# Queries of a hybrid transformer block from seven half-size products, with combined operands made by accumulating transfers

## The chip, the cores and the metric

The kernel runs on one core of a Trainium2 chip. The metric is device time in microseconds (us). Lower is better.

## What is computed

One layer of a diffusion backbone on 1024 latent tokens and 256 context tokens of 1024 features, in float32. In short (the MLP and the second half of the layer are left out; the change doesn't touch what they compute):

```python
h_x = _modulate(x, g_pre_mix[l], sh1, sc1)          # rmsnorm(x) * gain * (1 + scale) + shift
h_c = _modulate(ctx, g_pre_mix[l], csh1, csc1)
u_x, q_x, k_x, v_x = _project(h_x, w_in[l])         # h @ w_in, four blocks of 512 columns
u_c, q_c, k_c, v_c = _project(h_c, w_in[l])
attn_x = _neighbourhood_attention(q_x, k_x, v_x, k_c, v_c, rpb[l])
mix_x = jnp.concatenate([_pool_mixer(u_x, pool_w[l], pool_scale[l]), attn_x], axis=-1) @ w_out[l]
x = x + gt1 * _rmsnorm(mix_x, g_post_mix[l])
```

The pool mixer takes, in four groups of 128 channels, a sliding mean over 2, 4, 8 or 16 tokens less the token itself, and multiplies it with a 128 x 128 matrix. The attention has 8 heads of 64 features; the shift, scale and gate vectors come from a product of silu(c) with w_mod, 1024 x 6144. The queries are the product of the 1024 x 1024 modulated tokens with 512 columns of w_in, times -1/8 as the kernel keeps them.

## The kernel before

**Precision and tiles.** Each factor of a float32 product is split into a high part (rounded to the matmul's type, by ACT) and a low part (the rest, subtracted by DVE), and each product of two tiles is three matmuls (`three`, L193 to L196): high x high, high x low, low x high. The modulated tokens stand feature-major: `hx[b][k]` is one page of 128 x 1024 elements for half b of the tokens (512) and features 128k to 128k + 127, its left half the high part, its right half the low part. A page is a buffer of the pool `act`, of which there are 33 (L89). Raw weights go through 4 buffers (`wraw`), split weights through 8 (`whl`), so one group of 512 columns of w_in, split, fills all 8.

**Order of the work around the change.** After a start in which the tokens are normalised, turned and modulated, and the keys are formed, come: the context's keys (`pkc`, L565); the values of the context (`pvc`) and of eight tiles of latent tokens (`pv`, L575 to L593); the pool mixer's projection in eight groups (`pu`, L651 to L670), each followed by DVE work on the sliding sums (`pooled`), whose result is split at once into the pages `d`; the queries (`queries`, L704), eight groups `pq{j}_{b}` of 24 matmuls for feature tile j and token half b; and the pool products (`pool_out`, L638: three matmuls for each group and half, then evacuations to `y` and `mix`). Four query groups of token half 0 come first, then `pq0_1`, then the pool products, then `pq1_1`, and the last two groups stand in the first two turns of attention. In between run `background` steps: sums over w_mod for the later vectors, each step one load of 512 KB and one operation of DVE (L209 to L217), some number of them after each group.

**Attention** (L926 on) is a software pipeline over 32 units (head pair j, column block m). A turn forms scores (PE), adds the bias table and takes the maximum (DVE), exponentiates (ACT), turns the result (PE) and multiplies with the values (PE). The bias tables `tab` are made by POOL from a mask and the loaded position bias (L684).

**What sets the order.** A planner orders each engine's instructions from their program order and their readiness in its own time model, hands out buffers and puts in the waits. Inside `in_order(...)` the named engines keep the program's order: PE in the part that starts with `pq0_1` and the pool products (`pooling`), PE, ACT, DVE and SP in attention and before the values. Loads go through SP's queue; accumulating transfers (`add_to`: the destination is read, added to and written by the DMA) through POOL's.

Of the kernel before, what the change touches and what calls it, by code (L numbers as in the profile page):

```python
# [80 lines left out]
def hybrid_block(ctx, tc, x, ctx_in, w_mod, b_mod, gp1, gp2, w_in, pool_w, rpb, w_out, w1, w2, vectors,  # L81
# [61 lines left out]
    def split(src, hi, lo):  # L143
        nc.scalar.copy(hi, src)
        nc.vector.tensor_tensor(lo, src, hi.bitcast(F32), sub)
# [9 lines left out]
    def step_split(src, hi, lo, less=False):  # L155
        if less:
            nc.scalar.activation(hi, src, AF.Copy, scale=-1.0)
        else:
            nc.scalar.copy(hi, src)  # L159

        def second():
            if less:
                nc.vector.scalar_tensor_tensor(lo, src, -1.0, hi.bitcast(F32), mul, sub)
            else:
                nc.vector.tensor_tensor(lo, src, hi.bitcast(F32), sub)  # L165

        if stepwise:
            behind.append(second)
        else:
            second()  # L170
# [6 lines left out]
    def high_low(name, raw):  # L177
        hi = whl.tile([P, 1024], F32R, tag="hl", name=f"{name}h")
        lo = whl.tile([P, 1024], F32R, tag="hl", name=f"{name}l")
        split(raw, hi, lo)  # L180
        return hi, lo

    def weights(name, src):
        return high_low(name, load(name, src))
# [13 lines left out]
    def modulated(tmp, name, src, scale, shift, hi, lo, n, on_act=False):  # L198
        h = tmp.tile([P, 512], F32, tag="t", name=f"{name}t")
        if on_act:  # L200
            nc.scalar.activation(h[:, :n], src, AF.Identity, bias=shift, scale=scale)
            nc.scalar.copy(hi, h[:, :n])
        else:
            nc.scalar.activation(hi, src, AF.Identity, bias=shift, scale=scale)
            nc.vector.tensor_scalar(h[:, :n], src, scale, shift, mul, add)
        nc.vector.tensor_tensor(lo, h[:, :n], hi.bitcast(F32), sub)
# [49 lines left out]
    with tc.tile_pool(name="ps1", bufs=6, space=PSUM) as ps1, tc.tile_pool(name="tmp1", bufs=3) as tmp:  # L256
# [39 lines left out]
        nc.vector.tensor_scalar_add(b_sc, b_sc, 1.0)  # L296
        sT = once("sT", [P, KT, 32])
# [100 lines left out]
        def shift_scale(q, mr):  # L398
# [5 lines left out]
            for v in range(2):  # L404
                nc.vector.tensor_tensor(a1[v][:, hs], pv[:, 1, v], b_sc[:, hs], add)
                nc.vector.tensor_tensor(a1[v][:, hs], a1[v][:, hs], g1c[:, hs], mul)
                nc.vector.tensor_tensor(s1[v][:, hs], pv[:, 0, v], b_sh[:, hs], add)
# [3 lines left out]
        def latent(b, k):  # L411
# [3 lines left out]
                      on_act=(b == 1))  # L415
# [50 lines left out]
        for q in range(4):  # L466
# [3 lines left out]
            if q < 3:  # L470
                mr = mod_rows(q + 1)
                wgt.append(high_low(f"wk{q + 1}", raw_k[q + 1]))
# [78 lines left out]
        def in_group(name, c0):  # L551
            return [weights(f"{name}{kk}", pair(w_in, kk, c0, 512)) for kk in range(KT // 2)]
# [11 lines left out]
        raw_v = [load(f"wv{kk}", pair(w_in, kk, 1536, 512)) for kk in range(KT // 2)]  # L564
# [1150 lines left out]
```

## Time before, and its profile

| | |
|---|---|
| time before, median of 3 runs | 1044.7 us (1044.54 to 1045.26) |
| the profiled execution's own time | 1044.82 us |
| its span, first to last instruction | 1043.0 us |
| PE, DVE, ACT, POOL busy | 99%, 68%, 51%, 9% of the span |
| start of the context's values | 88.1 us |
| start of the pool projection | 144.3 us |
| start of the queries | 189.4 us |
| start of the pool products | 216.7 us |
| first scores | 227.9 us |

The profile is of one execution. PE is the matmul engine, PEld its weight loads, DVE, ACT and POOL the elementwise engines, SP the engine that issues loads. A line number is one of the kernel's; where a helper records an operation (`three`, `split`), every use has the helper's line. "[7.08 <-PE pq L196]" behind a row says that the engine had been idle for 7.08 us before it and that the last thing it waited for was a matmul into `pq`. In a group's row the name before the arrow is written and those behind it are read.

### The profile page before, as it was taken

How to read it: one execution, taken by the hardware profiler on the slowest of the kernel's cores; microseconds unless marked ns; L12 is line 12 of the kernel's file. 1: busy time of each engine (PE TensorE's matmuls, PEld its weight loads, DVE VectorE, ACT ScalarE, POOL GpSimd, SP SyncE). 2: the span in 40 equal slices, each digit the busy share in tenths (PEclk: the TensorE clock that was granted, in tenths of full speed). 3: DMA queues.
4: the chain of work that ended last, by engine and by line, in shares of the span. 5: the costliest groups of instructions: out<-in, count | busy, mean ns of one | idle time of the engine just before them, and what ended most of it. 6: DMA issues, size and time to landing. Idle time of an engine off the chain costs nothing.

```text
span 1043.0 us, 15532 instructions
## 1 busy us (share of the span) xinstructions
PE 1029.6 (99%) x5862; PEld 846.0 (81%) x5862; DVE 711.6 (68%) x1118; ACT 530.8 (51%) x923; POOL 96.4 (9%) x155
## 2 busy tenths in 40 slices
PE   8999999999999999999999999999999999999996
PEld 6788788877888888887888888888888888888885
DVE  5535657536897588878998876764676666547586
ACT  7553121247888465876655555545553334334441
POOL 3010200041331203320000000000000000000001
PEclk9999999999999999999999999999999999999998
DMA  9905764033337696595786553445787766655556
GB/s 341 337 21 178 270 216 135 21 75 100 64 81 189 160 218 203 189 250 167 263 271 231 193 191 129 156 139 192 268 325 264 234 230 222 200 173 194 175 187 201
DMA packets 108155, 199.61 MB, mean 191 GB/s; under 512 B 8496, under 2 KB 45104, under 8 KB 108080
## 3 DMA queue, kind: packets, MB, share of 16 engines
q1 hardware_dynamic: 84544, 152.92, 44.7%
q10 hardware_dynamic: 17136, 30.97, 8.0%
q0 software_dynamic: 6400, 14.72, 6.7%
q8 instruction: 46, 0.75, 0.3%
q14 instruction: 29, 0.24, 0.1%
HBM read 149.81 MB, written 39.34 MB: 181 GB/s over the span
## 4 chain that ended last, share of the span: by engine, by line
PE 96%; ACT 1%; DMA 1%; DVE 1%; issue 0%; SPq 0%; DVEq 0%; POOLq 0%; ACTq 0%
PE pk L433 4%; PE S L753 3%; PE pa L829 3%; PE phv L194 3%; PE phz L194 3%; PE phx L194 3%; PE pyv L196 3%; PE phz L195 3%; PE pyz L196 3%; PE pyx L194 3%; PE phx L195 3%; PE phv L195 3%; PE pyx L196 3%; PE phx L196 3%; PE pyv L194 3%; PE pyz L195 3%
## 5 line engine op out<-in xcount | busy, mean ns | idle before, releaser
L140 POOL TENSOR_TENSOR ry<-vy,nhalf 128x1 f32<-128x1 f32 x8 | 4.4, 551 | 570.8 <-DVE vy L138 570.8
L776 ACT ACTIVATE sp<-sp,nm 128x640 f32<-128x640 f32 (+1 forms) x64 | 51.4, 803 | 9.5 <-DVE nm L767 8.7
L767 DVE CUSTOM_DVE_ANT_0 sp<-S,tab 128x640 f32<-128x640 f32 (+1 forms) x56 | 42.8, 802 | 17.9 <-PE S L753 11.3
L1328 ACT ACTIVATE c<-c 128x512 f32<-128x512 f32 x48 | 30.3, 632 | 46.2 <-DVE c L1448 21.6
L159 ACT CAST wpS<-S 128x512 fp32r<-128x512 f32 x64 | 38.6, 616 | 27.8 <-PE phv L196 9.4
L165 DVE TENSOR_TENSOR wpS<-S,wpS 128x512 fp32r<-128x512 f32 x64 | 43.5, 686 | 10.4 <-ACT wpS L159 10.4
L194 PE MATMUL phx<-thB,wpA 128*128 128x512 f32 x128 | 50.2, 392 | 0.0
L195 PE MATMUL phx<-tlB,wpA 128*128 128x512 f32 x128 | 49.8, 389 | 0.0
L196 PE MATMUL phx<-thB,wpA 128*128 128x512 f32 x128 | 49.8, 389 | 0.0
L1329 ACT ACTIVATE c<-c 128x512 f32<-128x512 f32 x48 | 30.3, 631 | 15.3 <-DVE sa L1411 12.1
L194 PEld LDWEIGHTS phx<-thB,wpA 128*128 128x128 f32 x128 | 24.0, 188 | 5.5 <-ACT s L1379 0.5
L753 PE MATMUL S<-kT,q 64*128 64x384 f32 (+1 forms) x128 | 28.0, 495 | 0.4 <-DVE nm L767 0.4
L196 PEld LDWEIGHTS phx<-thB,wpA 128*128 128x128 f32 x128 | 24.0, 188 | 5.1
L195 PEld LDWEIGHTS phx<-tlB,wpA 128*128 128x128 f32 x128 | 24.0, 188 | 4.8
L829 PE MATMUL pa<-pt,v 128*64 128x128 f32 x352 | 25.9, 279 | 0.7 <-ACT px L809 0.3
L814 DVE COPY pt<-T 128x512 f32<-128x512 f32 x32 | 21.9, 685 | 5.5 <-PE T L795 5.5
L194 PE MATMUL phz<-thB,wpS 128*128 128x512 f32 x64 | 25.0, 391 | 0.0
L194 PE MATMUL phv<-thT,wpA 128*128 128x512 f32 x64 | 25.0, 391 | 0.0
L196 PE MATMUL phv<-thT,wpA 128*128 128x512 f32 x64 | 24.9, 389 | 0.0
L195 PE MATMUL phz<-tlB,wpS 128*128 128x512 f32 x64 | 24.9, 389 | 0.0
L194 PE MATMUL phy<-thT,wpS 128*128 128x512 f32 x64 | 24.9, 389 | 0.0
L195 PE MATMUL phy<-tlT,wpS 128*128 128x512 f32 x64 | 24.9, 389 | 0.0
(1039 smaller groups left out, 3326.3 us busy)
## 6 DMA issues: line engine op xcount, KB each, us to landing
b<-in_w SPq DMA_DIRECT2D x64, 512.0 KB, 4.3
hrS<-hdS SPq DMA_DIRECT2D x32, 512.0 KB, 5.5
hrA<-hdA SPq DMA_DIRECT2D x24, 512.0 KB, 5.6
wm<-in_w_mod SPq DMA_DIRECT2D x16, 512.0 KB, 9.6
wa_0w<-in_w SPq DMA_DIRECT2D x16, 512.0 KB, 5.1
wa_1w<-in_w SPq DMA_DIRECT2D x16, 512.0 KB, 4.2
hdA<-c ACTq DMA_DIRECT2D x32, 256.0 KB, 2.4
hdS<-sa ACTq DMA_DIRECT2D x32, 256.0 KB, 2.6
```

Source lines behind the costliest of these rows:

```text
L159: nc.scalar.copy(hi, src)
L165: nc.vector.tensor_tensor(lo, src, hi.bitcast(F32), sub)
L194: nc.tensor.matmul(ps, ahi, bhi, start=first, stop=False, skip_group_check=more)
L195: nc.tensor.matmul(ps, ahi, blo, start=False, stop=False, skip_group_check=more)
L196: nc.tensor.matmul(ps, alo, bhi, start=False, stop=last, skip_group_check=more)
L433: nc.tensor.matmul(pks[b][j], wk(wgt, k, low, j * P, P), r, start=(k == 0 and n == 0), stop=(k == KT - 1 and n == 2))
L753: nc.tensor.matmul(S[e][:, c0 : c0 + keys.shape[1]], q[hs, cols], keys[hs], start=True, stop=True)
L767: nc.vector.tensor_tensor_reduce(out=to, in0=s, in1=bt, scale=1.0, scalar=BIG, op0=add, op1=ALU.min, accum_out=nm)
L776: nc.scalar.activation(sp, sp, AF.Exp, bias=least[i, e], scale=-1.0, accum_out=sums[i][:, e : e + 1])
L829: nc.tensor.matmul(pa[e * HD : (e + 1) * HD, cols], v[:, f : f + HD], turns[i][:, e, c] if c < 4 else fifths[i][:, :, (e + 1) * HD : (e + ...
L1328: nc.scalar.activation(r, src, AF.Relu)
L1329: nc.scalar.activation(r, r, AF.Square)
```

## The change

The query product is divided in halves three ways. The tokens give four blocks Abk, b the half of the tokens and k the half of the features (512 x 512 each); w_in's query columns give four blocks Bkc, k the half of the features and c the half of the 512 columns. Instead of eight products of blocks, seven are formed (Winograd's form of Strassen's scheme), from

- S1 = A21 + A22, S2 = S1 + A11, S3 = A21 + A11, S4 = S2 + A12, and T1 = B12 + B11, T2 = B22 + T1, T3 = B22 + B12, T4 = T2 + B21, where the second half of the features is kept with its sign turned (in tokens and weights both), which makes differences into sums;
- the products A11 x B11, A12 x B21, S2 x T2, S1 x T1, S4 x B22, S3 x T3, A22 x T4, each of 24 matmuls of 128 x 128 x 512, in this order.

For the sums, the modulated tokens are kept as plain float32 in place (`kept`), written to memory (`tokens`, 8 transfers of 512 KB), and read back into two pages for each S, the further terms added by accumulating transfers. S4 adds S2's raw pages, which lie in the chip's buffer already. The T are formed likewise from w_in in raw weight buffers. Each S is split into four pages. The first five products stand before the pool products in the in-order part; S3 x T3 and A22 x T4 stand in the first two turns of attention, where two query groups stood; `pq1_1` between the pool products and the first scores is gone. The evacuations add or subtract on DVE where they were a scaled copy on ACT.

The pool projection is moved ahead of the values. The values take token half 1 first. The pool differences are kept whole (`differences`) and split only next to the pool products, a group at a time (`difference_split`). Background steps come three at a time in the pool groups and context values, two in the first value groups. One small set of vector operations (`a2`, `less_a2`, `less_s2`) is put behind attention on DVE.

```diff
+    def add_to(to, more):
+        nc.gpsimd.dma_start(to, more, accum_op=add)
...
             modulated(tmp, f"hx{b}_{k}", src, a1[0][:, k : k + 1], s1[0][:, k : k + 1], h[:, :512], h[:, 512:], 512,
-                      on_act=(b == 1))
+                      on_act=(b == 1), kept=src if b == 1 or k > 1 else None)
...
-                wgt.append(high_low(f"wk{q + 1}", raw_k[q + 1]))
+                wgt.append(high_low(f"wk{q + 1}", raw_k[q + 1], 1.0 if q == 0 else -1.0))
...
             if j == 3:
-                wgt = [high_low(f"wv{kk}", raw_v[kk]) for kk in range(KT // 2)]
+                wgt = in_weights("wu", raw_u)
             nc.scalar.copy(kc[:, j], ps)
+
+        tokens = dram.tile([P, KT, SEQ], F32, tag="tokens", name="tokens")
+        for k in range(KT):
+            if k < 2:
+                hi, lo = hx[0][k][:, :512], hx[0][k][:, 512:]
+                nc.vector.tensor_tensor(xT[k][:, :512], hi.bitcast(F32), lo.bitcast(F32), add)
+            nc.sync.dma_start(tokens[:, k], xT[k])
...
+                if g == 3 and b == 0:
+                    raw_v = in_raw("wv", 1536)
+                if g == 3 and b == 1:
+                    wgt = in_weights("wv", raw_v)
+                background(3)
+            differences.append(pooled(g, up).rearrange("p (r m c) -> p m r c", r=QR, m=NM))
...
+        def token_raw(name, first, *more):
+            raw = [page(f"{name}r{i}") for i in range(2)]
+            for i in range(2):
+                nc.sync.dma_start(two(raw[i]), token_half(first, i))
+            for m in more:
+                for i in range(2):
+                    if isinstance(m, str):
+                        add_to(two(raw[i]), token_half(m, i))
+                    else:
+                        add_to(raw[i], m[i])
+            return raw
+
+        def token_operand(name, raw):
+            rows_of[name] = []
+            for i in range(2):
+                hi, lo = page(f"{name}h{i}", F32R), page(f"{name}l{i}", F32R)
+                split(raw[i], hi, lo)
+                rows_of[name] += [(hi[:, o : o + 512], lo[:, o : o + 512]) for o in (0, 512)]
...
+        for n, m in enumerate((4, 5, 6, 7, 0, 1, 2, 3)):
+            ps = bank(f"pv{m}")
+            token_group(ps, wgt, lat_tok(m // 4, m % 4))
...
+            background(2)
+            if n == 2:
+                sraw["S2"] = token_raw("S2", "A21", "A22", "A11")
+            if n == 3:
+                qraw["B11"] = query_raw("B11", "B11")
+                qraw["B21"] = query_raw("B21", "B21")
+                qraw["T2"] = query_raw("T2", "B22", "B12", "B11")
+            if n == 5:
+                token_operand("S2", sraw["S2"])
+                qraw["T1"] = query_raw("T1", "B12", "B11")
...
-        for j in range(4):
-            queries(j, 0, bank(f"pq{j}_0"), (1, 2, 3, 99)[j])
-        mask_page()
-        tables(0)
         with in_order(ET.PE) as pooling:
-            queries(0, 1, bank("pq0_1"), 0)
+            w11, w21 = (query_weights(n, qraw[n]) for n in ("B11", "B21"))
+            x = [bank(f"pqx{j}") for j in range(2)]
+            for j in range(2):
+                query_product(x[j], j, "A11", w11, True)
+                nc.scalar.copy(query(j, 1), by_tile(x[j]))
+            wt = query_weights("T2", qraw["T2"])
+            qraw["B22"] = query_raw("B22", "B22")
+            sraw["S1"] = token_raw("S1", "A21", "A22")
+            for j in range(2):
+                query_product(x[j], j, "A12", w21, False)
+                nc.scalar.copy(query(j, 0), by_tile(x[j]))
+            wt1 = query_weights("T1", qraw["T1"])
+            token_operand("S1", sraw["S1"])
+            sraw["S4"] = token_raw("S4", "A12", sraw["S2"])
+            qraw["T3"] = query_raw("T3", "B22", "B12")
+            qraw["T4"] = query_raw("T4", "B21", "B22", "B12", "B11")
+            y = [bank(f"pqy{j}") for j in range(2)]
+            for j in range(2):
+                query_product(y[j], j, "S2", wt, True)
+                nc.vector.tensor_tensor(query(j, 1), by_tile(y[j]), query(j, 1), add)
+            wb22 = query_weights("B22", qraw["B22"])
+            token_operand("S4", sraw["S4"])
+            mask_page()
+            tables(0)
+            z = [bank(f"pqz{j}") for j in range(2)]
+            for j in range(2):
+                query_product(z[j], j, "S1", wt1, True)
+                nc.vector.tensor_tensor(query(2 + j, 1), query(j, 1), by_tile(z[j]), sub)
+            sraw["S3"] = token_raw("S3", "A21", "A11")
+            wt3 = query_weights("T3", qraw["T3"])
+            difference_split(0)
+            for j in range(2):
+                query_product(z[j], j, "S4", wb22, False)
+                nc.vector.tensor_tensor(query(2 + j, 0), by_tile(z[j]), query(j, 1), sub)
+            wt4 = query_weights("T4", qraw["T4"])
+            token_operand("S3", sraw["S3"])
             for g in range(4):
+                if g < 3:
+                    difference_split(g + 1)
                 pool_out(g)
...
             with tc.issue_after(pooling[ET.PE]):
-                queries(1, 1, bank("pq1_1"), 0)
+                pass
...
                 if i < 2:
-                    queries(2 + i, 1, bank(f"pq{2 + i}_1"), 0)
+
+                    for j in range(2):
+                        query_product(last_queries[j], j, ("S3", "A22")[i], (wt3, wt4)[i], i == 0)
+                    for j in range(2):
+                        to, less = (query(2 + j, 1), query(2 + j, 1)) if i == 0 else (query(j, 1), query(j, 1))
+                        if i == 0:
+                            nc.vector.tensor_tensor(to, less, by_tile(last_queries[j]), sub)
+                        else:
+                            nc.vector.tensor_tensor(to, by_tile(last_queries[j]), less, sub)
```

More of the change, by code (lines that the diff above doesn't have):

```diff
@@ L563, in hybrid_block @@
         kc = kcp.rearrange("p (j t) -> p j t", j=4)
-        raw_v = [load(f"wv{kk}", pair(w_in, kk, 1536, 512)) for kk in range(KT // 2)]
+        raw_u = in_raw("wu", 0)
         for j in range(4):
@@ L673, in hybrid_block @@
+        background(99)
+        vb = [vp[m // 2][:, (m % 2) * 512 : (m % 2) * 512 + 512] for m in range(NM)]
         tabs, msk = [], []
```

141 lines of the change are left out of this document (78 added, 63 removed).

## The prediction

> **What bounds the kernel now.** I read the page's busy table first, then the granted clock, then busy time by stretch around the change, and last the timelines of PE, ACT and DVE and the waits of the queues there.
>
> ```profile
> span 1043.0 us, 15532 instructions
> PE 1029.6 (99%) x5862; PEld 846.0 (81%) x5862; DVE 711.6 (68%) x1118; ACT 530.8 (51%) x923; POOL 96.4 (9%) x155
> core 0: 1043.0 us, clock 0.997
> core 0: us, PE busy (x) PEld busy (x) DVE busy (x) ACT busy (x) POOL busy (x), PEclk, DMA share, GB/s
> 88.00:100.00 12.00, 12.00 (x55) 9.78 (x54) 9.27 (x9) 3.35 (x6) 0.00 (x0) 1.00 0.81 280
> 100.00:112.00 12.00, 12.00 (x59) 9.36 (x58) 9.88 (x8) 1.55 (x3) 0.45 (x1) 1.00 0.92 316
> ...
> 160.00:176.00 16.00, 16.00 (x73) 13.24 (x72) 13.91 (x25) 4.46 (x8) 0.00 (x0) 1.00 0.53 170
> 176.00:189.00 13.00, 13.00 (x64) 10.18 (x63) 4.64 (x9) 3.64 (x4) 1.91 (x4) 1.00 0.13 43
> 189.00:200.00 11.00, 11.00 (x50) 9.13 (x49) 9.06 (x27) 3.39 (x6) 0.00 (x0) 1.00 0.00 0
> 200.00:216.00 16.00, 16.00 (x73) 13.24 (x72) 7.49 (x9) 2.89 (x6) 1.19 (x4) 1.00 0.09 26
> ```
>
> PE has work in 99% of the span, at full clock, and in every stretch from the values to the queries it never waits (12.00 of 12.00, 16.00 of 16.00). The time is therefore the number of matmuls times their pitch, as long as operands stand ready. DMA is nearly full at 100 to 112 (0.92) and empty at 189 to 200 (0.00). A matmul fewer in this part is time saved; a late operand is time lost at once, since PE's order through the products is fixed and holds nothing to run in between.
>
> **The change part by part. Fewer matmuls.**
>
> ```profile
> 189.44 0.39 PE L194 MATMUL pq<-hx,wq0h 128*128 128x512 f32 x1
> ...
> 194.88 0.39 PE L194 MATMUL pq<-hx,wq0h 128*128 128x512 f32 x1
> ...
> 216.65 0.40 PE L194 MATMUL py<-d,pwh 128*128 128x512 f32 x1
> ...
> 222.33 0.39 PE L194 MATMUL pq<-hx,wq0h 128*128 128x512 f32 x1
> ...
> 227.86 0.70 PE L753 MATMUL S<-kcT,q 64*128 64x256 f32 x4
> ```
>
> The first two rows are the starts of two query groups of 24 matmuls: 5.44 us, 0.2267 each (the 0.39 is latency, overlapped). Before: 8 groups, 192 matmuls. After: 7 products of 2 column tiles x 4 feature tiles x 3, 168. That is 24 x 0.2267 = 5.44 us less, all of it ahead of the first scores: before, six groups stood there, now five products; two groups or products follow in attention's first two turns in both. Nothing hides this gain, and the changed order of pools and values costs PE nothing, the same matmuls being issued. The first product thus starts where the first group does, at 189.44 on before's clock.
>
> **The pools ahead of the values.** The background sums now fall on the pool groups, three steps each, together with the pools' DVE work, the 8 writes of the tokens to memory, and the values' weights at the end.
>
> ```profile
> L194 PE MATMUL pvc<-wv0h,hc x4: 389/390/396, 88.1 to 94.4; 128*128 128x512 f32 x4
> ...
> 88.35 0.34 SPq L174 DMA_DIRECT2D wmsh_0w<-in_w_mod  x1
> ...
> 111.28 0.33 SPq L174 DMA_DIRECT2D wmsc_7w<-in_w_mod  x1
> ...
> 186.70 1.06 ACT L144 CAST wq1h<-wq1w 128x1024 fp32r<-128x1024 f32 x1 [0.32 <-PE pu L195]
> ...
> 187.79 1.23 DVE L145 TENSOR_TENSOR wq1l<-wq1w,wq1h 128x1024 fp32r<-128x1024 f32 x1 [0.15 <-ACT wq1h L144]
> ```
>
> Sixteen loads of 512 KB went out in 22.9 us, 1.53 us each, at 280 to 316 GB/s. Between 88 and the values I count 8 token writes, 19 background loads (22 steps, of which three only open a sum) and the 4 loads of the values' weights: 31 x 1.53 = 47.4 us, so the last lands near 135.8. Its split takes 1.06 + 1.23: 138.1. PE comes to this stage at 88.1 (the first row, the values' start before); eight groups end at 131.6, and the fourth weight is read 18 matmuls (4.1 us) later, at 135.7. So PE waits 2.4 if transfers only follow one another, and nothing if the writes find gaps; I take half, 1.2. The upper end is some 9, if DVE (9.88 of 12.00 busy already) works off its queue of sums and pools late, with the weights' subtractions behind them.
>
> **Operands by adding transfers.** S1, S2, S4, S3 are each loaded in two tiles and added to by DMAs of POOL's queue, then split on ACT and DVE into four pages; T1 to T4 likewise in weight buffers. A second accumulation waits in POOL's queue for the first, and whatever is queued there stands behind it (the bias tables among it).
>
> ```profile
> wq1w<-in_w_in SPq DMA_DIRECT2D x1, 512.0 KB, 4.6
> wq3w<-in_w_in SPq DMA_DIRECT2D x1, 512.0 KB, 3.7
> x<-xr POOLq DMA_DIRECT2D x8, 512.0 KB, 4.3
> nf<-nf POOLq DMA_DIRECT2D x2, 512.0 KB, 6.4
> nf<-t POOLq DMA_DIRECT2D x2, 512.0 KB, 8.8
> to_1w<-in_w_out POOLq DMA_DIRECT2D x1, 512.0 KB, 13.2
> ```
>
> A load takes 3.7 to 4.6, I take 4.1. An accumulation: 6.4 and 8.8 for a few at a time, 13.2 on full DMA; a plain store from the same queue 4.3. I take 7.6, midway between the two rows of the same kind and size, keep 4.3 and 13.2 as ends, and 2.3 for ACT and DVE to split. S2, T2 and T1 are ordered in the middle of the values, more than 25 us ahead: I cost them at nothing, DMA having room there (0.53, then 0.13 busy). What counts is when pages come free.
>
> ```profile
> SPq L677 <- PE pq L196: 25.9, 1, 25.9
> POOL tab L682 <- PE pq L196: 24.8, 1, 24.8
> 206.64 1.23 DVE L612 TENSOR_TENSOR sa<-u 128x1023 f32<-128x1023 f32 x1 [7.08 <-PE pq L196]
> ```
>
> Before is already short of its 33 pages here: the mask's load stood 25.9 us and the tables' memset 24.8 until a query group had read its last token page, and a pool sum 7.08. After has more to hold. At the first product I count 12 token pages (A11, A12, A22), 10 of keys and values, 4 differences, 6 of S2: 32 of 33, and the last goes to the queries. So S1's tiles wait for A11's pages, given free by the 15th and 18th matmul of the first product, at 192.8 and 193.5. First half of S1: 192.8 + 4.1 + 7.6 + 2.3 = 206.8; its product is due at 189.44 + 3 x 5.44 = 205.76, its second half, 207.5, is due 6 matmuls later at 207.1. Wait 1.0, product done at 212.2. S4's second tile takes a page of S2, read for the last time 18 matmuls into the third product, 204.4: 204.4 + 4.1 + 7.6 + 2.3 = 218.4, wanted 6 matmuls into the fifth product, 212.2 + 1.4 = 213.6. Wait 4.8. Together 5.8; with 4.3 for an accumulation 2.5, with 13.2 some 11.5.
>
> The Trainium skill ("DMA: Bandwidth & Descriptors", section "Anatomy of one DMA — SWDGE (gpsimd) path") fits 2.0 us plus bytes / 436e3 for such a DMA, 3.2 us here. The rows of accumulations, 6.4 to 13.2, don't agree; by the page the two waits would be about 1.4 and the whole 4.4 us better, 1045.7, which falls in the even case below.
>
> **The pools' products and the first scores.** Before, the pool products (216.65 to 222.33) are followed by a query group of 5.44 us, and the evacuations run on beneath it.
>
> ```profile
> 223.72 0.75 DVE L649 SCALAR_TENSOR_TENSOR mix<-py,cols,mix 128x512 fp32r<-128x512 f32 x1 [0.99 <-ACT mix L648]
> ...
> 218.95 0.69 ACT L645 ACTIVATE y<-py,npcol 128x512 f32<-128x512 f32 x1
> ...
> 225.24 0.77 ACT L645 ACTIVATE y<-py,npcol 128x512 f32<-128x512 f32 x1
> ...
> 213.11 1.14 ACT L144 CAST d<-sa 128x512 fp32r<-128x512 f32 x2 [15.11 <-DVE sa L628]
> ```
>
> ACT is done at 226.0, 3.7 us after PE, and the scores begin at 227.86, unharmed. After, the scores follow the pool products at once, and they take PSUM banks that those products have just filled. What hid 3.7 us is gone. Besides, the differences are split here, group by group, since the pages allow no more: three groups of two casts, 1.14 a group, 3.4 us more on ACT if none lies ahead. Bounds: 1.6, if the scores' four banks aren't those of the last pool group (its three evacuations of about 0.69 then don't count), and 7.1, with the casts. I take 3.7.
>
> The other edits have one answer: query evacuations turn from ACT into DVE adds, about 0.75 us each by the DVE row above, which reads PSUM too, while PE runs the next product; negated weights and shifts change the form, not the count; tokens kept in place need no new instruction but two adds; the two last products use two banks of their own. I cost these at nothing; DVE is idle 5.42 us in either of attention's first turns.
>
> ```profile
> 235.97 0.82 DVE L767 CUSTOM_DVE_ANT_0 sp<-S,tab 128x640 f32<-128x640 f32 x1 [5.42 <-PE S L753]
> ```
>
> If that cover went, four adds of 0.75 would cost at most 3.0 us.
>
> **Sum.** The profiled execution took 1044.8 (span 1043.0 and 1.8 around it), the median of the runs is 1044.7. -5.4 + 1.2 + 5.8 + 3.7 = +5.3, so 1050.1.
>
> **The rivals.** *The gain comes through.* If the planner gives S1 and S4 their pages before S2 holds its six, or accumulations land at the plain store's 4.3 and loads overlap, both operands are there in time. It decides at S1 split before 205.8 and S4 before 212.6. Left is the bare bank wait of 1.6: -5.4 + 1.6 = -3.8, 1041.0. For it: DMA is empty from 189 on. Against: a page shortage that before's waits show already, and accumulation rows of 6.4 and up.
>
> *The differences wait for S3.* Before the second group's difference may be split, the program asks for S3's four pages; then its own page can be one that S3's second raw tile gives back: 218.4 + 4.1 + 7.6 + 2.3 = 232.4. Three more groups follow at about 2.5 each (two casts, a subtraction, three matmuls on one half), so the scores start at 240 instead of 227.86: +12, about 1057. For it: the same page count. Against: pages of the tables' source and of the first difference may come first.
>
> *Even.* Waits of 3.3 to 7.5 eat the gain: 1044.7 to within 2.1.
>
> The Trainium skill ("TensorE: Matmul & The Clock Gate", section "Part 1: The HAM clock gate (the "warmup" mystery)") says that an idle window of about 3.4 us halves the clock until as long a window of work is past. Before has no wait so long in mid-kernel, so no row here tells; by that rule the wait of 4.8 would cost some 1.7 more, 1051.8.
>
> **How the numbers follow.** The forecast (operands and banks late) gets 0.48, its own range 1047 to 1055; the gain coming through 0.25; the differences behind S3 0.17; even 0.10. Each measured against 0.2%, 2.1 us, about what runs of this kernel can tell from no change: faster 0.25, same 0.10, slower 0.48 + 0.17 = 0.65. The range for 8 in 10 goes from 1040.5, just under the first rival, to 1059.5: the sum with accumulations of 13.2 comes to 1055.8, and the late values or S3's pages bring some 4 more.
>
> **What the profile would show.** Right: 168 matmuls into the query tiles at 0.2267 pitch; PE idle before the S1 and the S4 product, released by the DVE subtraction of a split; PE idle before the first scores, released by ACT's evacuations; SP's loads of S1 and S4 waiting for PE. Wrong: PE at 99% up to the scores and a span 4 to 5 us shorter, or the idle time in another place (at the values' first weights, or between the pool groups).

## The result, and the profile after

The changed kernel takes 1103.3 us (median of six runs, 1099.9 to 1105.3) against 1044.6 us before: ratio 1.0557, 95% interval 1.0540 to 1.0575. The forecast had the side right, slower, and the size wrong: +5 us were expected, +59 came, far above the range. The profiled execution took 1101.5 us; all comparisons of places in the span below are with it.

The head of the page of the changed kernel, with the granted clock in 40 slices of 27.5 us:

```profile
span 1099.6 us, 15610 instructions
PE 1039.7 (95%) x5838; PEld 849.4 (77%) x5838; DVE 729.9 (66%) x1142; ACT 539.2 (49%) x930; POOL 117.9 (11%) x172
PEclk9999789977999999999999999999999999999999
```

PE executes 24 instructions fewer than before (5838 against 5862) and is still busy 10 us longer, over a span that grew by 56.6. The third row, the granted clock in tenths, bears on that: slices 5, 6, 9 and 10, which hold the pools, the first values and the query products, ran below full clock. From slice 11 on it shows 9 throughout.

What PE waited for in the changed kernel, the longest rows (us in total, times, longest):

```profile
PE pgsh L227 <- DVE accsh L220: 14.0, 1, 14.0
PE pqz L198 <- ACT S1h L146: 9.6, 2, 6.3
PE pga L227 <- issue: 8.0, 1, 8.0
PE pqz L198 <- DVE q L824: 6.2, 1, 6.2
PE py L198 <- ACT d L146: 5.2, 2, 4.6
PE S L867 <- DVE mix L648: 2.1, 1, 2.1
```

Two of the six waits, 22.0 us together, are of a kind that the prediction does not mention. `pgsh` and `pga` are the small matmuls that reduce the background sums over the partitions. The other four are the ones it named: S1, S4 (released here by the row that came last, the evacuation of the product before), the pool differences, and the first scores.

Busy time by stretch shows where the two halves of the loss lie, with the starts of the first product and the first scores:

```profile
core 0: us, PE busy (x) PEld busy (x) DVE busy (x) ACT busy (x) POOL busy (x), PEclk, DMA share, GB/s
104.00:120.00 16.00, 2.00 (x12) 0.76 (x11) 14.22 (x16) 1.45 (x3) 0.00 (x0) 0.67 0.85 273
...
176.00:215.00 39.00, 39.00 (x178) 31.73 (x177) 5.60 (x6) 7.56 (x11) 10.90 (x11) 1.00 0.84 179
215.00:238.00 23.00, 17.00 (x76) 13.73 (x74) 5.30 (x5) 6.26 (x9) 6.25 (x5) 0.95 0.90 211
238.00:258.00 20.00, 9.58 (x24) 6.18 (x24) 9.09 (x9) 5.86 (x7) 6.13 (x10) 0.67 1.04 215
258.00:284.00 26.00, 17.55 (x56) 12.11 (x56) 12.70 (x18) 13.71 (x22) 8.66 (x16) 0.76 0.52 106
```

```profile
L198 PE MATMUL pqx<-hx,wqB11h x8: 389/389/389, 215.5 to 220.3; 128*128 128x512 f32 x8
L867 PE MATMUL S<-kcT,q x128: 376/376/480, 282.9 to 388.9; 64*128 64x256 f32 x128
```

Before, the first query group started at 189.4 and the scores at 227.9. So 26.1 us are lost ahead of the first product, 28.9 more between it and the scores (67.4 instead of 38.5), and 1.6 behind them. In the stretch of the values, 176 to 215, PE is full at full clock: nothing is lost there. Between 104 and 120 it is DVE that is full (14.22 of 16.00) while PE does almost nothing. Between 238 and 258 neither DVE nor ACT is full: there the splits of S1 and S4 wait for transfers, and PE for the splits. The last 3.4 us of S4's wait are DVE's order: its first half is split at 254.9, but the evacuation that must read the product's bank first stands on DVE behind the second half's split, at 257.51.

The rows behind the first wait, from the timelines of POOL and SP's queue, DVE's sums and PE:

```profile
97.02 0.95 POOL L215 MEMSET accsh<- 128x1024 f32 x1 [31.10 <-DMA tokens<-xT]
92.24 7.99 SPq L590 DMA_DIRECT2D tokens<-xT  x8
100.33 1.15 SPq L178 DMA_DIRECT2D wmsh_3w<-in_w_mod  x1
L220 DVE SCALAR_TENSOR_TENSOR accsh<-wmsh_0w,sx,accsh x1: 1283/1283/1283, 103.7 to 103.7; 128x1024 f32<-128x1024 f32 x1
L220 DVE SCALAR_TENSOR_TENSOR accsh<-wmsh_7w,sx,accsh x1: 1284/1284/1284, 117.2 to 117.2; 128x1024 f32<-128x1024 f32 x1
118.50 1.08 PE L227 MATMUL pgsh<-accsh,ones 128*32 128x256 f32 x8 [14.00 <-DVE accsh L220]
```

The sum cannot begin before its page is zeroed, and that page is one that a token tile holds until it is written to memory. The eight writes also stand in SP's queue between the sum's third and fourth load, so that the fourth goes out at 100.33. The planner's order on PE has the reduction behind the third pool group, at 104.5; the sum's eight steps on DVE lie among the pools' work until 118.5.

The rows behind S1 and S4, from POOL's timeline and the DMA issues (KB each, median us to landing):

```profile
222.66 1.29 POOL L188 DMA_DIRECT2D wqT3w<-in_w_in  x1 [17.89 <-DMA wqT3w<-in_w_in]
224.37 1.27 POOL L188 DMA_DIRECT2D wqT4w<-in_w_in  x1 [0.42 <-issue]
225.71 1.18 POOL L188 DMA_DIRECT2D S1r<-tokens  x1
234.86 1.29 POOL L188 DMA_DIRECT2D wqT4w<-in_w_in  x1 [7.97 <-DMA wqT4w<-in_w_in]
235.62 1.74 POOL L188 DMA_DIRECT2D S1r<-tokens  x1
...
246.85 0.86 POOL L188 DMA_DIRECT2D S4r<-S2r  x1 [3.72 <-DVE S1l L152]
```

```profile
S1r<-tokens POOLq DMA_DIRECT2D x2, 512.0 KB, 10.0
S4r<-S2r POOLq DMA_DIRECT2D x2, 512.0 KB, 9.6
```

The prediction took 7.6 for an accumulation. S1's first half goes out as soon as its load has landed, among the first ones of T3 and T4, and lands after 11.4 us, the second after 8.6; S4's take 10.9 and 8.2. And S1's second half stands in POOL's queue behind T4's second accumulation, which waits 7.97 us for T4's first: it is issued at 235.62, ten us behind S1's first half.

### The profile page after: what moved, and what is told of

The parts are those of the page before. It is cut to its first block, busy times and chain, and to the rows that moved or that the text cites. A ratio compares the mean times of both kernels' runs of the same rounds, so it can differ in the third digit from the quotient of the medians.

```text
span 1099.6 us, 15610 instructions
## 1 busy us (share of the span) xinstructions
PE 1039.7 (95%) x5838; PEld 849.4 (77%) x5838; DVE 729.9 (66%) x1142; ACT 539.2 (49%) x930; POOL 117.9 (11%) x172
## 3 DMA queue, kind: packets, MB, share of 16 engines
q0 software_dynamic: 12560, 23.64, 11.4%
## 4 chain that ended last, share of the span: by engine, by line
PE 83%; DMA 6%; ACT 3%; issue 3%; DVE 2%; POOL 1%; SPq 1%; ACTq 0%; DVEq 0%; POOLq 0%
PE pk L442 4%; PE S L867 3%; PE pa L943 3%; PE pyv L198 3%; PE pyz L198 3%; PE pyx L199 3%; PE pyx L198 3%; PE pyv L200 3%; PE pyz L200 3%; PE pyv L199 3%; PE pyz L199 3%; PE pyx L200 3%; PE phv L198 3%; PE phz L198 3%; PE phz L199 3%
## 5 line engine op out<-in xcount | busy, mean ns | idle before, releaser
L152 DVE TENSOR_TENSOR wpS<-S,wpS 128x512 fp32r<-128x512 f32 x64 | 43.5, 685 | 10.5 <-ACT wpS L146 10.5
L780 POOL TENSOR_TENSOR tab<-msk,U 128x128 f32<-128x128 f32 x48 | 21.6, 487 | 44.1 <-DMA U<-in_rpb 44.1
L198 PE MATMUL phz<-thB,wpS 128*128 128x512 f32 x64 | 25.0, 391 | 0.1
L200 PE MATMUL phz<-thB,wpS 128*128 128x512 f32 x64 | 24.9, 389 | 0.0
```

The costliest lines, as they stand in the source:

```text
L198: nc.tensor.matmul(ps, ahi, bhi, start=first, stop=False, skip_group_check=more)
L200: nc.tensor.matmul(ps, alo, bhi, start=False, stop=last, skip_group_check=more)
```

## The experiments

Four causes were open after the result: that the background's reductions stand too early in PE's order; that the token writes and adding transfers, with the pages and the queue they take, make what is behind them late; that only POOL's order of the additions does; and that the slow clock is a cost of its own. The runs that edit the changed kernel and the reorder alone have one time each, compared with the 1101.5 of the profiled execution; the changed kernel's own times spread over 5 us, so differences of a few us say nothing there. In the expectations TensorE is PE, VectorE DVE, ScalarE ACT and GpSimd POOL.

**Closings later.** The reductions run three background calls after their sum.

```diff
-            while closing:
-                closing.pop(0)()
+            calls[0] += 1
+            while closing and (closing[0][0] + 3 < calls[0] or n == 99):
+                closing.pop(0)[1]()
...
+            closing.append((calls[0], close))
```

> The changed kernel with one edit: the four reductions of the background sums (matmuls into pgsh, pgsc, pga, pgb) stand three background calls later in the program. Theory A (PE's fixed order reaches a reduction before its sum is done): pgsh comes after the sixth pool group instead of the third, at about 121 us, when the sum, done at 118.4 in the changed kernel, is there; pga comes after the second value group. The waits of 14.0 and 8.0 us go, with the slow clock behind them (about 4 us): 1074 to 1078 us instead of 1101.5. Theory B (the sums are only the first to show that DVE and DMA are late): the wait moves to the values' weights, and the time stays above 1090.

1090.6 us. PE's longest waits in this kernel:

```profile
PE pqx L198 <- ACT q L802: 10.6, 1, 10.6
PE pqz L198 <- DVE q L825: 9.3, 1, 9.3
PE pvc L198 <- ACT wv0h L146: 7.0, 1, 7.0
PE py L198 <- ACT d L146: 5.1, 1, 5.1
PE pgsh L227 <- issue: 2.4, 1, 2.4
```

The two waits of 22.0 us shrink to 2.4, and the time falls by only 11: the values' weights are now late by 7.0 (the wait that the prediction had named, and that the earlier waits had covered). The second query product waits 10.6 for a copy that ACT does behind T1's split, and ACT itself stands 13.24 us there for T1's transfers. So the time is at the border of theory B's range: the two waits are real, but about half of them covers others. Neither theory holds alone; both do in part.

**Sums in buffers of their own.**

```diff
+        def sum_page(name):
+            return tmp.tile([P, 1024], F32, tag="acc", name=name, bufs=2)
...
-            for acc in mod_sum(name, c, page, sx):
+            for acc in mod_sum(name, c, sum_page, sx):
```

> The changed kernel, with the sums behind the pools' reductions (accsh, accsc, acca, accb) in two buffers of their own instead of two pages of the shared ring; nothing else differs. Theory G (pages): the memset of accsh waits 31.1 us because the pages of the ring are held by the tokens until their write to memory is done, so the sum begins at 103.7 us, and TensorE waits 14.0 us for it at pgsh. It should then begin 10 us earlier or more, the wait of pgsh fall to 2 to 5 us (2.4 where there are no token writes at all), and the span by 9 to 12 us: 1089 to 1093 us. Theory H (the sum's own loads or VectorE's queue are late, the page only seems to be the cause): the wait stays over 10 us and the time within 3 us of 1101.5.

1096.6 us, `pgsh` waits 9.8 instead of 14.0: in neither theory's ranges. The memset now runs at 1.5 us and the first sum at 92.9, as early as before the change (92.3). The pages are 4 us of the wait. The rest begins with a load:

```profile
107.81 1.29 DVE L220 SCALAR_TENSOR_TENSOR accsh<-wmsh_3w,sx,accsh 128x1024 f32<-128x1024 f32 x1 [1.24 <-DMA wmsh_3w<-in_w_mod]
```

Behind the third of eight steps, at 96.64, DVE works on the pool groups and stands idle; the fourth waits for its load, which SP's queue issues at 100.73, behind the eight token writes (92.42, 8.21 us), and which lands 7.1 us later. In the reorder alone, below, which has no writes, the same load goes out at 91.67 and the fourth step runs at 97.73. So theory H is right in kind on the rest, the sum's own loads are late, and it is the writes that make them so.

**The reorder alone.** The kernel before, with the pool projection ahead of the values, the background steps at three and two, and the differences split late; queries in eight groups, no tokens in memory, no additions. The values keep their order of tokens.

```diff
+                if g == 3 and b == 1:
+                    wgt = [high_low(f"wv{kk}", raw_v[kk]) for kk in range(KT // 2)]
+                background(3)
+            differences.append(pooled(g, up).rearrange("p (r m c) -> p m r c", r=QR, m=NM))
...
+        for m in range(NM):
...
+            background(2)
...
+            difference_split(j)
```

> The kernel before with one part of the change: pool projection ahead of the values, background steps 3, 3 and 2 a group as in the change, differences split late; queries in eight groups, no token writes, no additions. Theory A: PE reaches pgsh at 104.5 us, and the sum, not held up by token pages, is done at about 106 to 108; pga still stands behind sums whose loads wait for the values' weights to leave the four buffers, some 8 us: 1053 to 1059 us. Theory E (the token writes alone make the sums late): within 2 us of 1044.6.

1060.1 us, 15.4 above before, just over the 1053 to 1059 expected of the reorder. All of it lies ahead of the first query group, which starts at 204.8 instead of 189.4. Its longest waits:

```profile
PE pga L223 <- issue: 9.2, 1, 9.2
PE pgsh L223 <- DVE accsh L216: 2.4, 1, 2.4
```

So `pga`'s wait belongs to the reorder, and nearly all of `pgsh`'s does not. Why `pga` waits stands in SP's queue of the changed kernel: `wma_2` is issued at 130.88, then the values' weights take the four raw buffers at 133.28 to 140.94, and the next load of the sum comes at 147.59, when the first of these weights has been split. Its last five steps then take turns with the pools' sums on DVE until 162.8. In the reorder alone the values' weights take the buffers from 121.44, and the next load of the sum goes out at 136.78.

**No additions, then no writes either.** First every accumulating transfer is left out, so that each S and T holds its first term only; then also the writes of the tokens, with the two sums of halves ahead of them, and the loads of the S read blocks of w_in instead.

```diff
-            for m in more:
-                for i in range(2):
-                    if isinstance(m, str):
-                        add_to(two(raw[i]), token_half(m, i))
-                    else:
-                        add_to(raw[i], m[i])
```

> The changed kernel without any accumulating transfer for S1 to S4 and T1 to T4: each is only its first term, so the query products are of other numbers; all else stays. Theory C (the additions' time and queue): the stretch from the first product to the first scores falls from 67.4 us to 45 or less, 1079 us or less in all; what is left there is the pool evacuations and the pages. Theory D (pages): the stretch stays above 58, 1092 or more.

1078.3 us. PE's longest waits, and the first scores:

```profile
PE pgsh L227 <- DVE accsh L220: 15.7, 1, 15.7
PE pga L227 <- issue: 8.4, 1, 8.4
PE py L198 <- ACT d L146: 3.5, 2, 2.8
```

```profile
L859 PE MATMUL S<-kcT,q x128: 376/376/480, 261.3 to 366.0; 64*128 64x256 f32 x128
```

All waits at S1 and S4 are gone (pool differences and first scores still wait, some 6 us), and the stretch from the first product (216.5) to the scores is 44.8 us instead of 67.4. The additions cost 23 us. The second step:

```diff
-            return tokens[:, 4 * kh + 2 * i : 4 * kh + 2 * i + 2, b * 512 : (b + 1) * 512]
+            return pair(w_in, 2 * kh + i, b * 512, 512)
...
-            nc.sync.dma_start(tokens[:, k], xT[k])
```

> The run without additions (1078.3 us), and also without the eight writes of the tokens to memory and the two sums of halves ahead of them: the loads of S1 to S4 read blocks of a weight of the same size instead of tokens, so the sums of tokens and of weights and the tokens themselves are left out of S and T. Order, products, splits and loads stay. Theory O (the writes are what makes the first reduction late: they hold pages, VectorE and the queue in the stretch where the sums begin): the wait of pgsh falls from 15.7 us to 2 to 5 us, as in the reorder alone (2.4), and the time to 1064 to 1068 us. Theory P (the three steps a group are enough to make it late, writes or not): pgsh waits 8 us or more and the time stays over 1070 us.

1067.4 us, in the range of theory O:

```profile
PE pga L227 <- issue: 7.8, 1, 7.8
...
PE pgsh L227 <- DVE accsh L220: 2.1, 1, 2.1
```

The writes, with the pages and the queue that they hold, cost 11 us; the wait of `pgsh` falls by 13.6, and the first product starts at 202.9.

**POOL in the program's order.**

```diff
-        with in_order(ET.PE) as pooling:
+        with in_order(ET.PE, ET.Pool) as pooling:
```

> The changed kernel with POOL kept in program order through the products: the additions into S1 and S4 are issued before those into T3 and T4. Theory C (the second half of S1 waits in POOL's queue behind T4's serial additions): the second S1 addition is issued within 2 us of the first instead of 9.9 us later; PE's waits before and in the S1 product fall from 10.5 us to about 6, those for S4 by some 3: about 1092 us. Theory D (pages decide): S1's and S4's raw tiles are asked for no earlier, and the time stays within 4 us of 1101.5.

1107.7 us. S1's waits fall from 10.5 to 2.8 us, and those at S4 and the pool products grow to 9.1 and 15.6. That S1 was held up by the others' additions is shown: its first half, going out ahead of them, lands after 6.1 us instead of 11.4. But POOL's order alone mends nothing: T3 and T4 now come later, and the evacuation that S4's product waits for stands on DVE behind T3's split, the casts of the differences on ACT behind T4's. We take it that there are too many additions for one queue in this stretch; other orders of ACT and DVE were not tried in this kernel.

**Pool products ahead of S4's product.**

```diff
             difference_split(0)
+            for g in range(4):
+                if g < 3:
+                    difference_split(g + 1)
+                pool_out(g)
             for j in range(2):
                 query_product(z[j], j, "S4", wb22, False)
...
-            for g in range(4):
-                if g < 3:
-                    difference_split(g + 1)
-                pool_out(g)
```

> The changed kernel with S4xB22 moved behind the pool products, so that TensorE takes S1xT1, the pool products, S4xB22 and then the first scores; two of the pools' banks come from the lasting ones, nothing else differs. In the changed kernel S4's operand comes at 258 us, TensorE waits 6.3 us for it, and then 8.3 us inside and behind the pool products. Theory M (S4's operand comes when its transfers land, whatever TensorE does before): the pool products fill that wait and S4's matmuls hide the pools' evacuations: first scores at 268 to 274 us instead of 282.9 and 1088 to 1093 us. Theory N (the pool products' own operands are late because ScalarE and VectorE split them between those of S1 and S4): the pool products wait as long in their new place and the time stays within 4 us of 1101.5.

1103.3 us, theory N: the pool products wait 14.3 us for their own operands in the new place, S4's wait is gone, and the scores start at 286.2. Filling a wait with other work helps only if that work's operands are ready, and these come from the same two engines, ACT and DVE.

**The waits filled.** The clock is taken for itself.

```diff
+    def warm(name, n):
...
+        ps = lasting(f"warm{name}")
+        for _ in range(n):
+            nc.tensor.transpose(ps[:, :P], ident, ident)
```

> The changed kernel, with spare transposes of the identity (about 0.117 us each, onto a bank that nobody reads) put into TensorE's order where it waits: 115 ahead of pgsh, 64 ahead of pga, 54 ahead of the first and 54 ahead of the third of S1's and S4's products and 40 inside the pool products. They fill waits and compute nothing that is used. Theory I (the clock is a cost of its own): the granted clock, 0.974 in the changed kernel, goes back to about 0.997, the matmuls behind the waits run at the full rate, and the time falls by 8 to 15 us to 1087 to 1093 us although every operand comes as late as before. Theory J (the 48 us of waits are the whole cost, the clock is only seen beside them): the time stays within 3 us of 1101.5, or rises where the filling outlasts a wait.

```profile
core 0: 1098.1 us, clock 0.991
```

```profile
PE pqz L198 <- ACT S1h L146: 5.5, 2, 4.5
```

1099.9 us. The clock rises from 0.974 to 0.991, the row above is the largest wait that PE has left, and the time stays within 3 us: theory J. The first product starts at 213.2 instead of 215.5, the first scores at 280.6 instead of 282.9: what is gained, 2.3 us, is gained ahead of the products, where PE has full work behind each wait, and nothing among them. Our reading is that there matmuls that run slowly between two waits only shorten the next wait, since the operands come at their own time.

**First scores behind the pool products.** In the kernel before, one query group is moved ahead of the pool products.

```diff
+            queries(1, 1, bank("pq1_1"), 0)
             for g in range(4):
                 pool_out(g)
...
-                queries(1, 1, bank("pq1_1"), 0)
+                pass
```

> The kernel before, with one query group (pq1_1) moved from behind the pool products to ahead of them, so that the first scores follow the pool products with nothing between, as in the changed kernel; no work is added or removed. The prediction's last term: the evacuations of the pool products and the split of the first score's operands are then no longer hidden behind these 24 matmuls, which costs 3.7 us (bounds 1.6 to 7.1): 1046.3 to 1051.8 us, most likely 1048.4. Rival: VectorE and ScalarE keep up with the pool products as they go, and it costs nothing measurable: 1042.6 to 1046.8 us. If it costs more than 7 us the term was mis-sized by the order alone.

1050.5 us against 1044.8, ratio 1.0061 (1.0047 to 1.0074), that is 5.7 us by the medians, 4.9 to 7.7 by the interval. The profiled run shows one wait of 3.8 us of the scores on DVE's `mix`, near the 3.7 of the prediction; the other 2 us were not followed. The term is real and was taken somewhat low.

**The sums on DVE.** Three kernels form S1 to S4 from the split halves in the chip's buffer, with before's order of pools and values. In the first POOL adds the T.

```diff
+            for to, more in (("B11", "B12"), ("B12", "B22"), ("B22", "B11"), ("B21", "B22")):
+                nc.gpsimd.tensor_tensor(qraw[to], qraw[to], qraw[more], add)
...
+            token_add(sum_of, sum_of, "A11")
+            token_operand("S2", sum_of)
```

> Before's order (values ahead of the pools, before's pattern of background steps) with the seven products of the changed kernel in another form: no token is written to memory and no transfer adds. VectorE forms A21+A22 and the further sums of tokens from the split halves that are in SBUF already, GpSimd adds the weights' blocks in place from four plain loads, and TensorE takes P1, P2, S1xT1, S2xT2, then the pool products, then S4xB22, then the first scores; the rest of the products stands where before's last query groups stood. Theory K (the 24 matmuls are worth what they cost wherever no operand is late, and the changed kernel lost its time to lateness): 5.4 us come off, 1039 to 1042 us if VectorE's sums stay hidden. Theory L (the sums of tokens cannot be hidden at this place on any engine: 32 additions of 512 columns on VectorE queue ahead of the splits that the products wait for): waits of 5 us or more show at S1's product or at the pool products and the time is 1045 us or more.

1067.2 us, ratio 1.0218 (1.0204 to 1.0232). PE waits 12.8 us between the first two products, for a copy that ACT does behind the splits of three operands not needed yet, and 4.8 at the pool products. From DVE's and POOL's timelines:

```profile
186.62 1.23 DVE L153 SCALAR_TENSOR_TENSOR wqB11l<-wqB11w,wqB11h 128x1024 fp32r<-128x1024 f32 x1 [0.64 <-ACT wqB11h L147]
187.99 3.41 DVE L153 SCALAR_TENSOR_TENSOR wqB21l<-wqB21w,wqB21h 128x1024 fp32r<-128x1024 f32 x1
```

```profile
187.93 2.39 POOL L769 TENSOR_TENSOR wqB11w<-wqB11w,wqB12w 128x1024 f32<-128x1024 f32 x1 [29.09 <-DVE wqB11l L153]
190.40 3.26 POOL L769 TENSOR_TENSOR wqB12w<-wqB12w,wqB22w 128x1024 f32<-128x1024 f32 x1
```

The same DVE operation takes 1.23 us ahead of POOL's additions and 3.3 to 3.4 beside them. The second kernel adds the T on DVE, keeps ACT's and DVE's order, and forms A21 + A22 among the values:

```diff
-        with in_order(ET.PE) as pooling:
+        with in_order(ET.PE, ET.Activation, ET.DVE) as pooling:
+            def weight_sum(to, more):
+                nc.vector.tensor_tensor(qraw[to], qraw[to], qraw[more], add)
```

> The form of v2_sums_on_vector (1067.2 us) with its three delays mended: the weights' blocks are added on VectorE and not on GpSimd (beside GpSimd's four additions VectorE's operations of 1024 columns took 3.3 us instead of 1.23), ScalarE and VectorE keep the written order, so that the copies of P1 go ahead of later splits, and A21+A22 is formed in the stretch of the values. TensorE's order is P1, P2, S1xT1, A22xT4, S2xT2, the pool products, scores, and S3xT3 and S4xB22 beside the first scores. Theory K (the 24 matmuls come through where nothing is late): 1038 to 1042 us, waits before the first scores under 2 us. Theory L (VectorE cannot take some 30 additions more between 186 and 222 us, where it had 14 us of 36 free): waits of 4 us or more at S2xT2 or the pool products, 1044 to 1052 us, no better than before.

1070.2 us, ratio 1.0241 (1.0224 to 1.0258): neither range. The first scores start at 234.4, 13 us earlier than in the first kernel, yet PE then waits 8.3 us among them for S3, after 7.7 for T4 ahead of them:

```profile
PE pqf L194 <- ACT wqT4h L147: 7.7, 1, 7.7
PE pqv L194 <- ACT S3h L145: 4.9, 2, 4.4
PE pqv L195 <- DVE S3l L151: 3.4, 2, 2.9
```

The third puts T4's split ahead of S2 and S3's and S4's sums among the scores:

```diff
+                if i == 0:
+                    s3raw = [page(f"S3r{k}") for k in range(2)]
+                    token_add(s3raw, sums2, "A22", sub)
+                    token_operand("S3", s3raw)
```

> The form of v3_sums_earlier (1070.2 us), where TensorE waited 7.7 us at A22xT4 because VectorE formed S2 ahead of T4's split, and 8.3 us at S3xT3 because S3's and S4's sums stood ahead of the first scores. Here T4 goes ahead of S2, T2 is formed in B11's buffer so that B22 is split late, ScalarE copies S2's raw sum into two pages, and S3 and S4 are formed from these behind the first and the fourth unit of scores, their products behind the third and the seventh. Theory K (what is left of the loss is these two queues, and the 24 matmuls come through without them): 1040 to 1044 us. Theory L (VectorE is the limit from 186 to 222 us, so the wait only moves to S2xT2 or the pool products, and the sums among the scores delay the scores): 1046 to 1058 us. Over 1060: neither, and the waits will name another cause.

1083.2 us, ratio 1.0369 (1.0352 to 1.0386), over 1060 as its last sentence allowed for. The wait of 7.7 at T4 is gone, and the pool products start at 222.4 instead of 227.6; the loss is now before and among the scores, the longest waits:

```profile
PE S L843 <- DVE nm L857: 8.0, 3, 6.0
PE S L843 <- DVE mix L682: 7.4, 1, 7.4
```

None of the three beats the kernel before. Each removed the wait that it was made for and got another; eight additions of 0.68 us (512 columns) are 5.4 us of DVE, as much as the 24 matmuls that all of this saves, and over 30 are needed. Whether a fourth arrangement would come out below 1044.7 was not tried.

## Why the prediction was wrong, point by point

**Fewer matmuls, -5.4: right.** The first two products run without a gap from 215.5 to 226.4, 48 matmuls in 10.9 us, 0.227 each. PE has 24 instructions fewer. The gain is there; it is a tenth of what it is set against.

**"The changed order of pools and values costs PE nothing", +1.2 for the values' weights: wrong, +26.1.** This step failed first. It counted PE's matmuls and the transfers and left out that four background reductions stand in PE's planned order: with three steps a group PE reaches them before DVE has the sum. The reorder alone costs 15.4 us, with 9.2 of wait at `pga`; the token writes bring another 11, through the wait at `pgsh`. The prediction counted the writes as transfers only: they also hold the page of the sum (4 us of that wait) and stand in SP's queue ahead of the sum's loads. The text on record names idle time between the pool groups as a sign of being wrong, and that is where the 14.0 us came. The wait that it did name, for the values' weights, is hidden behind these and shows as 7.0 us once they are gone (closings later), below its upper end of 9, and as 0.7 in the reorder alone, which has no writes. The count of 31 transfers at 1.53 us assumed that loads follow one another; in fact four raw buffers tie each load to the DVE step that frees its buffer.

**Adding transfers, +5.8: the right places, the size wrong, 23 us.** The load of S1 went out 3.6 us after the first product's start, where the prediction had 3.4; three weight loads stand right ahead of it in SP's queue, so that the page need not be what set it. The step that failed is the cost behind that: the additions of T3 and T4 were put at nothing for S1, though they share its queue and its time. S1's first half then took 6.1 us to load and 11.4 to add, where 4.1 and 7.6 were assumed; with POOL in the program's order the same addition took 6.1. Its second half, assumed to go out as soon as its load had landed, stood in the queue until 235.62. At S1 PE waited 10.5 us instead of 1.0, at S4 6.2 instead of 4.8. Of the other 6 of the 23 us some 2 lie behind the first pool product (16.8 us to the scores, 14.7 without additions); the rest was not split up.

**Pool products and scores, +3.7: right in kind, low.** By itself it is 5.7 (4.9 to 7.7). In the changed kernel the stretch from the first pool product (266.1) to the scores (282.9) is 16.8 us, where before's pool products alone took 5.7. Three of the four differences are split there beside S3: 8.1 us of waits, and the rest partly at a lower clock.

**The clock rule.** The Trainium skill ("TensorE: Matmul & The Clock Gate", section "Part 1: The HAM clock gate (the "warmup" mystery)") was cited for 1.7 us on top. The trace agrees: behind the 14.0 us at `pgsh` the granted clock is 0.50 from 118.5 to 122.0, and matmuls start 0.43 us apart there instead of 0.23, some 1.6 us in all, estimated from these rows. But with all waits filled the gain came to about 2 us in all: the slow clock costs little where the next operand is late anyway.

**The rivals.** "The differences wait for S3" names the right place, the splits of the differences, for about +12 at the first scores; it is one of several here and does not stand for the loss. The second group's cast goes out on ACT at 271.60, directly behind S3's second (270.65), which had waited for S3's additions; so ACT's order is enough to explain it, and the page that the rival names is not needed. "The gain comes through" would have needed S1 split 16.4 us after the first product's start; its product waited until 22.8 us after it.

**The ledger.** From single runs, in this order, beside before's 1044.7: reorder 15.4; additions 23.2 (1101.5 to 1078.3); writes 10.9 (to 1067.4). What is left between 1067.4 and the reorder alone, 1060.1, is 7.3: the saved 5.4 against 12.7 for the rest, of which 5.7 is the place of the scores, if it costs here what it costs by itself. The other 7.0 was not isolated; 4.2 us of waits at the pool products and the lower clock around them lie in that stretch, and some 3 us are lost behind the first scores. So the side, slower, was forecast for reasons that are real but carry less than half of the loss (23.2 and 5.7 of 58.7 us).

## What to carry to other kernels

When a stage moves, list everything that stands in the full engine's order, the small matmuls of background work too, and ask for each when its operand is ready in the new place, and what stands in the queue ahead of its loads; a busy engine at 99% shows none of these deadlines. An algebraic saving of matmuls must pay for the additions on whatever engine or queue makes them, with the buffers they hold: here 5.4 us against 34. And a wait is worth only what it does not hide: here 22 us of waits, taken away, gave 11.

## What the runs showed of the hardware

DVE is slowed by POOL's work beside it: 1024-column operations of two operands took 1.23 us on DVE alone and 3.3 to 3.4 beside POOL's additions. POOL's own took 2.4 and 3.3; what they take alone no run shows. The Trainium skill ("SBUF — State Buffer", section "SBUF: two separate sides") states that the two share a port pair as an exclusive lock for the whole instruction; the trace agrees, with some 2.1 us added to each DVE operation of two operands of 1024 columns in that stretch.

An accumulating transfer of 512 KB from POOL's queue took 5.8 to 11.4 us to land between 215 and 260 us, with other transfers under way, where the plain store of the same size from that queue took 4.2 in the median. The mean granted clock was 0.67 of full in stretches where PE stood for 6 to 14 us, and filling the waits with spare transposes brought the mean back to 0.991 without a gain that the runs can tell.
